# Stick-breaking attention of a streaming encoder step: four chains a head pair, softplus by absolute value, and projections placed behind named transposes

## The chip, the cores and the metric

The kernel runs on one core of one Trainium2 chip. The metric is the device time in microseconds (us) of one execution of the whole program, the median of several runs. A profile is one more execution, recorded by the hardware; its span runs from its first to its last recorded instruction.

A core has engines that run side by side, each with a queue that it takes in order: TensorE (PE, matmuls and transposes, with PEld for its weight loads), VectorE (DVE), ScalarE (ACT), GpSimd (POOL) and SyncE (SP, which here only starts DMA transfers). Operands lie in SBUF; TensorE writes to PSUM, eight banks of 128 x 512 floats.

## The reference: what is computed

A two-layer encoder takes one step for 512 prompt tokens and 8 running streams of 16 tokens (T = 640 rows of 1024). Each layer is half an FFN, a mixer, half an FFN. The change lies in the first layer's mixer, in its attention of 8 heads of 64 columns. The prompt has only its own keys; a running stream also has 256 cached keys and values.

```
def sb_block(q_blk, q_pos, k, v):
    z = einsum('bqhd,bkhd->bhqk', q_blk, k) * (SB_HEAD_DIM ** -0.5)
    mask = arange(k.shape[1])[None, :] < q_pos[:, None]
    sp = where(mask, softplus(z), 0.0)
    suffix = cumsum(sp, axis=3, reverse=True) - sp
    w = where(mask, exp(log_sigmoid(z) - suffix), 0.0)
    return einsum('bhqk,bkhd->bqhd', w, v)
...
    proj = x @ w_in                       # u for the S5 part; q, k, v
    g = gelu(ys + d_skip * u)             # ys: the S5 recurrence
    s5_out = g * sigmoid(g @ w_glu + b_glu)
    out = concatenate([s5_out, sb_out]) @ w_out
```

Since log_sigmoid(z) = z - softplus(z), a weight is exp(z - the sum of softplus from this key to the last).

## The kernel before

**Products.** Every fp32 projection is three products of fp32r halves: `split` (L93) casts the high part on ScalarE (L94) and subtracts it on VectorE (L95); `mm3` (L128) multiplies high by high, low by high and high by low (L133). `load_w` loads a weight and splits it.

**Attention.** The eight heads are four pairs p. `in_qk(p)` (L1050) projects a pair's q and k: each of the two weights takes 24 matmuls of 256 columns, then 24 of 384. `attend(p, i)` is the chain of prompt queries 128i to 128i+127, of n = 128(i+1) keys, both heads at once: scores (L962) and mask (L965) into two PSUM banks z; softplus in four steps (min on VectorE L951, Exp and Ln on ScalarE through `act_fn` L82, max on VectorE L954); a suffix sum for each head (L970); z minus the sums (L972); Exp; transposes back into z (L977); a copy to SBUF on ScalarE (L978); the weighted sum of the values (L981). Four such chains a pair, of 2 x 128 to 2 x 512 columns. `sample(p)` is the running streams' chain: their new keys are turned round by two matmuls with copies between (L995, L998); then come two halves f of four streams each, one after the other: scores (L1009, L1010, L1012), softplus, sum, subtraction, Exp, three transposes (L1021), a copy on VectorE (L1022); then the weighted sums of both (L1030, L1034), a copy (L1037) and transposes back (L1040, L1044).

**Places.** There are two z buffers of two banks each, three banks `a` for projections and one bank `o` for weighted sums. The cached keys `kc` have one buffer, the cached values `vc` three.

**Fill.** TensorE has other work to do while a chain runs on the other engines: `in_qk` of later pairs, the gate `s5_wglu` (8 groups of 12 matmuls), and the first half of the output projection, `out_half(0, t)` (10 groups of 12 matmuls of 512 columns, each added to `yacc` at L903). The second half, `out_half(4, t)`, needs the whole attention and ends the stage.

**Order.** A scheduler sets each engine's order before the program runs, by the program's order and by what waits for what; on the chip every engine takes its queue in that order. `tc.issue_after(x)` puts an instruction behind x in that order. In the kernel before nothing in this stage uses it.

Of the kernel before, what the change touches and what calls it, by code (L numbers as in the profile page):

```python
# [21 lines left out]
T = 640  # L22
# [13 lines left out]
def kernel(ctx: ExitStack, tc: tile.TileContext, I, O, phases=PHASES):  # L36
# [691 lines left out]
    def mixer0(ph, last):  # L728
# [167 lines left out]
        def out_half(k0, t):  # L896
            ks = range(k0, k0 + 4)
            for j in range(2):
                pb = bank_a()
                mm3(pb, [(xh[:, k, t * 128:t * 128 + 128], xl[:, k, t * 128:t * 128 + 128]) for k in ks],  # L900
                    [w_j(wo[k], j) for k in ks])
                ya = yacc[:, t, j * 512:j * 512 + 512]
                V.scalar_tensor_tensor(ya, pb, 1.0 / ALPHA, ya, op0=ALU.mult, op1=ALU.add)  # L903

        with ExitStack() as st:
# [50 lines left out]
            def attend(p, i, qT, kT, po):  # L956

                n = 128 * i + 128
                z = bank_z()
                for h in range(2):  # L960
                    rows = slice(64 * h, 64 * h + 64)
                    nc.tensor.matmul(z[:, h, :n], qT[rows, n - 128:n], kT[rows, :n],  # L962
                                     start=True, stop=False, skip_group_check=True)
                for h in range(2):
                    nc.tensor.matmul(z[:, h, n - 128:n], identb, negc, start=False, stop=True, skip_group_check=True)  # L965
                e = wk.tile([128, 2, 512], F32, name="es", bufs=4)
                S = wk.tile([128, 2, 512], F32, name="S", bufs=2)
                softplus_(e[:, :, :n], z[:, :, :n])
                for h in range(2):
                    V.tensor_tensor_scan(S[:, h, :n][:, ::-1], onec[:, 0:1].to_broadcast([128, n]),  # L970
                                         e[:, h, :n][:, ::-1], 0.0, op0=ALU.mult, op1=ALU.add)
                V.tensor_tensor(S[:, :, :n], z[:, :, :n], S[:, :, :n], op=ALU.subtract)  # L972
                act_fn(S[:, :, :n], S[:, :, :n], AF.Exp)

                for h in range(2):
                    for j in range(i + 1):
                        nc.tensor.transpose(z[:, h, 128 * j:128 * j + 128], S[:, h, 128 * j:128 * j + 128], ident)  # L977
                nc.scalar.copy(e[:, :, :n], z[:, :, :n])  # L978
                for j in range(i + 1):
                    for h in range(2):  # L980
                        nc.tensor.matmul(po[64 * h:64 * h + 64, n - 128:n],  # L981
                                         vt[:, j, 128 * p + 64 * h:128 * p + 64 * h + 64],
                                         e[:, h, 128 * j:128 * j + 128],
                                         start=(j == 0), stop=(j == i), skip_group_check=True)

            def sample(p, qT, kT):
# [6 lines left out]
                pk = bank("o")  # L993
                zs = bank_z()
                nc.tensor.transpose(pk[:, 0:128], kT[:, 512:640], ident)  # L995
                kk = wk.tile([128, 2, 128], F32, name="kk", bufs=1)
                nc.scalar.copy(kk[:, 0], pk[:, 0:128])
                nc.tensor.matmul(pk[:, 128:256], kk[:, 0], anti, start=True, stop=True)  # L998
                nc.scalar.copy(kk[:, 1], pk[:, 128:256])
                sp = wk.tile([128, 2, 512], F32, name="es", bufs=4)[:, :, :384]  # L1000
# [664 lines left out]
```

## Time and profile before

| | us |
|---|---|
| three runs, median | 2598.07 |
| lowest, highest | 2596.40, 2602.76 |
| the profiled execution, its time | 2599.58 |
| its span | 2597.9 |
| its mean granted TensorE clock | 0.988 |

The rows of the profile stand in a section below. The page's first line gives, for each engine, its busy time, its share of the span and its number of instructions. A window row gives the same for a stretch of time, with the granted clock (PEclk, 1.00 is 2.4 GHz, 0.50 is 1.2 GHz). Matmuls follow each other in a pipeline, so their single durations add up to more than the time they take; how long a series takes is read from its starts.

### The profile page before, as it was taken

The page shows a single profiled execution, that of the slowest core. Times are in us where ns is not written, and L with a number is a line of the kernel's source. Part 1 is how long each engine was busy: PE and PEld are TensorE (multiplying, and loading weights), DVE is VectorE, ACT ScalarE, POOL GpSimd, SP SyncE. Part 2 cuts the span into 40 slices and gives each one's busy share as a digit, 9 for nine tenths or more (in the row PEclk, how much of TensorE's full clock was granted, in tenths as well). Part 3 has the DMA queues.
Part 4 walks back from the last instruction along what each step waited for, and adds up shares of the span by engine and source line. Part 5 has one row for each costly group of instructions (what it writes and reads, how often), then busy time and mean ns, then how long its engine had stood idle before and what let it go on. Part 6 is the DMA issues. An engine that isn't in the chain of part 4 may idle for free. (4 is left out here: it accounts for less than half of the span.)

```text
span 2597.9 us, 40706 instructions
## 1 busy us (share of the span) xinstructions
PE 2522.9 (97%) x15577; PEld 2297.7 (88%) x15577; DVE 2038.0 (78%) x3728; ACT 1213.9 (47%) x2332; POOL 290.2 (11%) x412
## 2 busy tenths in 40 slices
PE   8999999999969999999999999999999999999998
PEld 8999998887648999998999999889899878999997
DVE  7788877667757988887888887777777698876768
ACT  4443444345534454554355554566565443443332
POOL 0000002110012000003000001411121151000001
PEclk9999999999979999999999999999999999999999
DMA  5332334542221244443144335355564622443442
GB/s 181 106 106 83 114 110 139 168 150 85 77 69 49 65 126 110 110 126 107 57 110 116 106 95 161 91 183 175 181 200 138 230 94 76 153 154 113 142 137 94
DMA packets 174835, 317.44 MB, mean 122 GB/s; under 512 B 20480, under 2 KB 91776, under 8 KB 174128
## 3 DMA queue, kind: packets, MB, share of 16 engines
q1 hardware_dynamic: 164816, 293.83, 35.5%
q0 software_dynamic: 9824, 21.01, 4.0%
q8 instruction: 122, 2.00, 0.3%
q14 instruction: 73, 0.60, 0.1%
HBM read 259.56 MB, written 40.54 MB: 116 GB/s over the span
## 5 line engine op out<-in xcount | busy, mean ns | idle before, releaser
L95 DVE TENSOR_TENSOR w<-raw,w 128x512 fp32r<-128x512 f32 (+1 forms) x617 | 537.0, 894 | 89.7 <-ACT w L94 87.7
L94 ACT CAST w<-raw 128x512 fp32r<-128x512 f32 (+1 forms) x617 | 451.1, 772 | 290.6 <-PE bank L133 111.3
L133 PE MATMUL bank<-xhi,w 128*128 128x256 f32 (+2 forms) x2528 | 557.6, 312 | 14.1 <-ACT xhi L94 6.9
L355 PE MATMUL bank<-xhi,w 128*128 128x320 f32 x2432 | 540.0, 309 | 1.7 <-ACT mx L366 1.4
L133 PEld LDWEIGHTS bank<-xhi,w 128*128 128x128 f32 x2528 | 423.1, 189 | 26.3 <-ACT xhi L94 8.0
L133 PE MATMUL bank<-w,h 128*128 128x512 f32 x1872 | 435.3, 391 | 0.8 <-DVE w L95 0.8
L355 PE MATMUL bank<-T,w 128*128 128x320 f32 x2736 | 426.3, 309 | 1.8 <-DVE s L392 1.3
L133 PEld LDWEIGHTS bank<-w,h 128*128 128x128 f32 x1872 | 349.3, 188 | 73.4 <-DVE w L95 1.2
L355 PEld LDWEIGHTS bank<-xhi,w 128*128 128x128 f32 x2432 | 407.4, 188 | 5.6 <-ACT mx L366 2.5
L355 PEld LDWEIGHTS bank<-T,w 128*128 128x128 f32 x2736 | 406.4, 188 | 3.6 <-DVE s L392 2.2
L133 PE MATMUL bank<-xlo,w 128*128 128x256 f32 (+2 forms) x1264 | 392.5, 311 | 6.4 <-DVE xlo L95 6.4
L355 PE MATMUL bank<-xlo,w 128*128 128x320 f32 x1216 | 375.0, 308 | 0.0
L133 PEld LDWEIGHTS bank<-xlo,w 128*128 128x128 f32 x1264 | 239.2, 189 | 8.9 <-DVE xlo L95 7.6
L355 PEld LDWEIGHTS bank<-xlo,w 128*128 128x128 f32 x1216 | 228.0, 188 | 0.3
L208 DVE SCALAR_TENSOR_TENSOR yacc<-bank,yacc 128x512 f32<-128x512 f32 x160 | 109.4, 687 | 76.3 <-PE bank L133 75.6
L366 ACT COPY mx<-bank 128x320 f32<-128x320 f32 x228 | 96.4, 423 | 141.4 <-PE bank L355 140.8
L95 DVE TENSOR_TENSOR w<-sw,w 128x1024 fp32r<-128x1024 f32 x76 | 93.0, 1224 | 53.2 <-ACT w L94 52.9
L94 ACT CAST w<-sw 128x1024 fp32r<-128x1024 f32 x76 | 79.8, 1050 | 101.2 <-DVE sw L334 100.0
L499 POOL DMA_DIRECT2D yacc<-ev x56 | 48.7, 903 | 651.5 <-ACT ev L498 597.5
L133 PE MATMUL bank<-w,og 128*128 128x512 f32 x432 | 106.3, 400 | 2.8 <-DVE og L1459 2.8
L133 PEld LDWEIGHTS bank<-w,og 128*128 128x128 f32 x432 | 80.7, 191 | 21.1 <-DVE og L1459 4.7
L394 ACT ACTIVATE s<-s 128x320 f32<-128x320 f32 x108 | 50.8, 470 | 85.3 <-DVE s L392 85.1
(418 smaller groups left out, 3317.7 us busy)
## 6 DMA issues: line engine op xcount, KB each, us to landing
raw<-in_w_gate_dram SPq DMA_DIRECT2D x88, 512.0 KB, 3.9
raw<-in_w_up_dram SPq DMA_DIRECT2D x88, 512.0 KB, 3.9
raw<-in_w_down_dram SPq DMA_DIRECT2D x88, 512.0 KB, 3.6
raw<-in_m_in_dram SPq DMA_DIRECT2D x52, 512.0 KB, 4.6
yacc<-ev POOLq DMA_DIRECT2D x56, 256.0 KB, 4.3
raw<-in_m_out_dram SPq DMA_DIRECT2D x24, 512.0 KB, 3.9
csb<-cs_d SPq DMA_DIRECT2D x20, 512.0 KB, 5.4
h<-in_ssd_h_dram SPq DMA_DIRECT2D x16, 512.0 KB, 6.1
```

What stands on the lines that cost most here:

```text
L94: nc.scalar.copy(hi, src)
L95: return nc.vector.tensor_tensor(lo, src, hi.bitcast(F32), op=ALU.subtract)
L133: state["pe"] = nc.tensor.matmul(ps, a, b, start=(k == 0), stop=(k == n - 1)).ins
L208: state["acc"] = nc.vector.scalar_tensor_tensor(ya, pb, scale, ya, op0=ALU.mult, op1=ALU.add).ins
L355: nc.tensor.matmul(ps, A[p][:, a, k * 128:k * 128 + 128], B[p][b][:, k, :], start=(first and n == 0), stop=(n == 11), skip_group_check=True)
L366: nc.scalar.copy(e[n], ps)
L394: state["silu"] = nc.scalar.activation(t, ps, AF.Silu).ins
L499: nc.gpsimd.dma_start(yacc[:, t, 512 * j:512 * j + 512], e, accum_op=ALU.add)
```

## The change

- **Chains.** A pair's prompt chains are now three: queries 384 to 511, queries 256 to 383, and the other two blocks side by side in one z buffer (256 + 128 columns a head). The two halves of the running streams are one chain of 2 x 384 columns. Below, u0, u1, u2 and the streams' chain (3 in `mark`) are a pair's four chains in order.
- **Softplus** is max(z, 0) + ln(1 + exp(-|z|)): Abs, Exp with scale -1 and Ln on ScalarE, and one fused operation on VectorE.
- **New keys** are turned round at the pair's start, in a bank `a`. The streams' copies are on ScalarE; their weighted sums go into the free columns of their own z banks. `kc` has two buffers, `es` three.
- **Fill.** `in_qk(1)` moves behind the first pair's chains in the program, `in_qk(2)` and `in_qk(3)` behind the first chain of pairs 1 and 2, and their groups, those of the gate and of the output's first half are each held behind the last transpose of a named chain.

```diff
+            def in_qk(p, places=None):
...
-                        nc.scalar.mul(t[:, o:o + L], cm_proj(wt, h)[:, :L], sc)
+                        with tc.issue_after(mark[places[0]]) if places and mark.get(places[0]) else ExitStack():
+                            pqk = cm_proj(wt, h)
+                        places = places and places[1:]
+                        nc.scalar.mul(t[:, o:o + L], pqk[:, :L], sc)
...
             def softplus_(e, z):
-                V.tensor_scalar_min(e, z, 40.0)
-                act_fn(e, e, AF.Exp)
+                nc.scalar.activation(e, z, AF.Abs)
+                act_fn(e, e, AF.Exp, scale=-1.0)
                 act_fn(e, e, AF.Ln, bias=1.0)
-                V.tensor_tensor(e, z, e, op=ALU.max)
+                V.scalar_tensor_tensor(e, z, 0.0, e, op0=ALU.max, op1=ALU.add)
...
+            def attend(p, u, parts, qT, kT, po):
+                n = sum(128 * i + 128 for i, _ in parts)
+                z = bank_z()
+                for i, o in parts:
+                    for h in range(2):
+                        rows = slice(64 * h, 64 * h + 64)
+                        nc.tensor.matmul(z[:, h, o:o + 128 * i + 128], qT[rows, 128 * i:128 * i + 128],
+                                         kT[rows, :128 * i + 128], start=(o == 0), stop=False, skip_group_check=True)
...
+                    for c in range(0, n, 128):
+                        mark[p, u] = nc.tensor.transpose(z[:, h, c:c + 128], S[:, h, c:c + 128], ident).ins
+                nc.scalar.copy(e, z[:, :, :n])
...
+            def new_keys(kT):
+                pk = bank_a()
+                nc.tensor.transpose(pk[:, 0:128], kT[:, 512:640], ident)
+                kk = wk.tile([128, 2, 128], F32, name="kk", bufs=2)
+                nc.scalar.copy(kk[:, 0], pk[:, 0:128])
+                nc.tensor.matmul(pk[:, 128:256], kk[:, 0], anti, start=True, stop=True)
+                nc.scalar.copy(kk[:, 1], pk[:, 128:256])
+                return kk[:, 1]
...
             in_qk(0)
-            in_qk(1)
             for p in range(4):
...
+                kr = new_keys(kT)
                 po = bank("o")
-                for i in range(4):
-                    attend(p, i, qT, kT, po)
+                for u, parts in enumerate((((3, 0),), ((2, 0),), ((1, 0), (0, 256)))):
+                    attend(p, u, parts, qT, kT, po)
+                    if (p, u) == (1, 0):
+                        in_qk(2, [(0, 2), (0, 3), (0, 3), (1, 0)])
+                    elif (p, u) == (2, 0):
+                        in_qk(3, [(1, 1), (1, 2), (1, 3), (2, 0)])
...
                 V.tensor_copy(qT[:, 0:512], po)
+                if p == 0:
+                    in_qk(1, [None, (0, 0), (0, 1), (0, 2)])
...
             wgl = [load_w(I["s5_wglu"][i]) for i in range(2)]
+            after = [mark[2, n] for n in (0, 1, 1, 1, 2, 2, 3, 3)]
...
+            after = [mark[p, n] for p, n in ((2, 3), (2, 3), (3, 0), (3, 0), (3, 1), (3, 1), (3, 2), (3, 2), (3, 3), (3, 3))]
             for t in range(NT):
-                out_half(0, t)
+                out_half(0, t, after)
```

The following rows are queues of instructions in the order in which TensorE takes them; several equal ones in a row are one row with their count. L133 is a projection (fill) in both kernels. In the changed kernel L968 and L972 are scores and masks, L986 a chain's transposes, L991 its weighted sum, L999 and L1002 the new keys, L1033 the streams' transposes, L1043 and L1047 their weighted sums, L1053 the transposes back.

**First pair.** TensorE before, around the first chain's transposes (L977, a chain of 2 x 128 columns); ahead of this piece stand 24 matmuls of fill:
```order
L133 MATMUL bank<-xhi,w 128x384 x2
L133 MATMUL bank<-xlo,w 128x384
L977 MATMUL bank<-ident,S 128x128 x2
L133 MATMUL bank<-xhi,w 128x384 x2
L133 MATMUL bank<-xlo,w 128x384
L981 MATMUL bank<-es,vt 64x128 x2
L962 MATMUL bank<-kT,qT 128x384 x2
L977 MATMUL bank<-ident,S 128x128 x4
L965 LDWEIGHTS identb
```

TensorE in the changed kernel, around the first chain's transposes; ahead of this piece stand the second chain's scores and masks and 21 matmuls of fill:
```order
L133 MATMUL bank<-xhi,w 128x256 x2
L133 MATMUL bank<-xlo,w 128x256
L986 MATMUL bank<-ident,S 128x128 x13
L991 MATMUL bank<-es,vt 64x128 x8
L986 MATMUL bank<-ident,S 128x128
L968 MATMUL bank<-kT,qT 128x256 x2
L968 MATMUL bank<-kT,qT 128x128
L991 MATMUL bank<-es,vt 64x128 x6
```

The first chain is now the widest, of 2 x 512 columns. Its eight transposes and the six of the second chain stand in a row, with the first chain's weighted sum and then the third chain's scores behind them and no fill between.

**Second pair.** TensorE before, ahead of the transposes of its third chain (2 x 384 columns), with 45 more matmuls of fill in front of this piece:
```order
L133 MATMUL bank<-xhi,w 128x256 x2
L133 MATMUL bank<-xlo,w 128x256
L977 MATMUL bank<-ident,S 128x128 x6
L133 MATMUL bank<-xhi,w 128x256 x2
L133 MATMUL bank<-xlo,w 128x256
L133 MATMUL bank<-xhi,w 128x256 x2
```

TensorE in the changed kernel, ahead of the transposes of its second chain (2 x 384 columns); in front of this piece stand the scores of the second and third chains:
```order
L972 LDWEIGHTS identb
L972 MATMUL bank<-negc,identb 128x128
L999 MATMUL bank<-ident,kT 128x128
L1002 MATMUL bank<-anti,kk 128x128
L986 MATMUL bank<-ident,S 128x128 x6
L133 MATMUL bank<-xhi,w 128x256 x2
L133 MATMUL bank<-xlo,w 128x256
L986 MATMUL bank<-ident,S 128x128 x3
L991 MATMUL bank<-es,vt 64x128 x6
```

The fill ahead of these transposes is gone from this place: all of the third pair's projections now stand in front of the second chain's scores. Ahead of the transposes there are only scores, masks and the new keys.

**The end.** TensorE before, from the last pair's third chain to the first half of its streams:
```order
L977 MATMUL bank<-ident,S 128x128 x6
L981 MATMUL bank<-es,vt 64x128 x6
L977 MATMUL bank<-ident,S 128x128 x8
L981 MATMUL bank<-es,vt 64x128 x8
L995 MATMUL bank<-ident,kT 128x128
L998 MATMUL bank<-anti,kk 128x128
L1009 MATMUL bank<-kk,qb 128x128
L1010 LDWEIGHTS identb
L1010 MATMUL bank<-negs,identb 128x128
L1012 MATMUL bank<-kc,qb 32x256 x4
L1021 MATMUL bank<-ident,es 128x128 x3
L1009 MATMUL bank<-kk,qb 128x128
```

TensorE in the changed kernel, around the last pair's streams' chain:
```order
L133 MATMUL bank<-w,xhi 128x512 x2
L1033 MATMUL bank<-ident,S 128x128 x6
L133 MATMUL bank<-w,xlo 128x512
L133 MATMUL bank<-w,xhi 128x512 x2
L133 MATMUL bank<-w,xlo 128x512
L1043 MATMUL bank<-vrev,es 128x128
L1047 MATMUL bank<-vc,es 32x128 x8
L1043 MATMUL bank<-vrev,es 128x128
L1047 MATMUL bank<-vc,es 32x128 x4
L133 MATMUL bank<-w,xhi 128x512 x2
L133 MATMUL bank<-w,xlo 128x512
L133 MATMUL bank<-w,xhi 128x512 x2
```

Before, no projection stands between the last chains' steps; now the output products of the first half stand around the streams' transposes and weighted sums.

## Rows read from the trace of the kernel before

**Rows 1.** The page's span and busy line: engine, busy us, share, instructions.
```profile
span 2597.9 us, 40706 instructions
...
PE 2522.9 (97%) x15577; PEld 2297.7 (88%) x15577; DVE 2038.0 (78%) x3728; ACT 1213.9 (47%) x2332; POOL 290.2 (11%) x412
```

**Rows 2.** Windows over the stage: stretch, us, busy by engine, PEclk, DMA.
```profile
570.80:584.60 13.80, 13.80 (x97) 13.61 (x96) 2.59 (x4) 3.80 (x8) 0.00 (x0) 1.00 0.44 139
584.60:722.60 138.00, 129.16 (x910) 96.79 (x909) 105.30 (x167) 79.88 (x150) 2.21 (x6) 0.98 0.26 80
722.60:759.60 37.00, 16.52 (x112) 10.05 (x112) 18.89 (x27) 12.24 (x20) 1.17 (x2) 0.57 0.32 101
759.60:803.70 44.10, 44.10 (x258) 38.62 (x257) 32.42 (x59) 16.12 (x25) 21.79 (x17) 0.98 0.12 34
```

**Rows 3.** VectorE's groups, 584 to 762: count | busy us, mean ns | idle before.
```profile
L970 DVE TENSOR_TENSOR_SCAN S<-onec,es 128x512 f32<-128x512 f32 x8 | 9.3, 1208 | 0.0
...
L970 DVE TENSOR_TENSOR_SCAN S<-onec,es 128x384 f32<-128x384 f32 x8 | 7.2, 942 | 0.0
L903 DVE SCALAR_TENSOR_TENSOR yacc<-bank,yacc 128x512 f32<-128x512 f32 x10 | 6.6, 683 | 0.8 <-PE bank L133 0.8
...
L951 DVE TENSOR_SCALAR es<-bank 128x1024 f32<-128x1024 f32 x4 | 4.9, 1214 | 0.5 <-PE bank L965 0.5
L954 DVE TENSOR_TENSOR es<-bank,es 128x1024 f32<-128x1024 f32 x4 | 4.8, 1208 | 0.0
...
L954 DVE TENSOR_TENSOR es<-bank,es 128x768 f32<-128x768 f32 x4 | 3.8, 953 | 3.6 <-ACT es L82 3.6
```

**Rows 4.** ScalarE's groups by shape, the same stretch.
```profile
L94 ACT CAST w<-raw 128x512 fp32r<-128x512 f32 x22 | 12.4, 615 | 1.6 <-PE bank L133 1.6
L82 ACT ACTIVATE es<-es 128x1024 f32<-128x1024 f32 x8 | 8.4, 1056 | 3.3 <-DVE es L951 3.1
L82 ACT ACTIVATE es<-es 128x768 f32<-128x768 f32 x8 | 6.7, 840 | 0.7 <-DVE es L951 0.5
...
L978 ACT COPY es<-bank 128x1024 f32<-128x1024 f32 x4 | 4.1, 1013 | 6.8 <-PE bank L977 6.8
```

**Rows 5.** TensorE's timeline: start us, us, what, output and operands, count.
```profile
570.80 0.39 PE L133 MATMUL bank<-xhi,w 128*128 128x256 f32 x2
...
577.68 0.39 PE L133 MATMUL bank<-xhi,w 128*128 128x256 f32 x2
...
580.41 0.51 PE L133 MATMUL bank<-xhi,w 128*128 128x384 f32 x2
...
584.66 0.49 PE L962 MATMUL bank<-kT,qT 64*128 64x128 f32 x4
...
586.03 0.48 PE L133 MATMUL bank<-xhi,w 128*128 128x256 f32 x2
...
762.23 0.39 PE L133 MATMUL bank<-w,xlo 128*128 128x512 f32 x1
...
764.97 0.39 PE L133 MATMUL bank<-w,xlo 128*128 128x512 f32 x1
```

**Rows 6.** Windows around stretches at the lower clock, columns as in Rows 2.
```profile
645.70:648.60 2.90, 2.90 (x20) 2.35 (x19) 2.39 (x6) 2.29 (x5) 0.00 (x0) 0.50 0.20 24
690.00:693.80 3.80, 3.80 (x17) 3.02 (x17) 0.96 (x2) 1.01 (x1) 0.00 (x0) 0.57 0.41 126
728.00:759.00 31.00, 14.37 (x91) 8.50 (x91) 13.48 (x20) 7.07 (x14) 1.17 (x2) 0.50 0.34 111
803.70:806.00 2.30, 0.07 (x1) 0.00 (x0) 1.42 (x4) 0.28 (x1) 0.00 (x0) 0.99 0.83 283
806.00:812.50 6.50, 3.89 (x12) 3.90 (x13) 3.92 (x9) 1.89 (x4) 0.00 (x0) 0.50 0.09 35
```

**Rows 7.** A wait of TensorE (timeline, idle in brackets); the cached values' landing.
```profile
808.61 1.97 PE L133 MATMUL bank<-xhi,w 128*128 128x384 f32 x5 [4.83 <-ACT xhi L94]
...
DMA to landing us min/median/max: 2.9/4.4/5.6
```

More of the change, by code (lines that the diff above doesn't have):

```diff
@@ L899, in out_half @@
                 pb = bank_a()
-                mm3(pb, [(xh[:, k, t * 128:t * 128 + 128], xl[:, k, t * 128:t * 128 + 128]) for k in ks],
-                    [w_j(wo[k], j) for k in ks])
+                with tc.issue_after(marks.pop(0)) if marks else ExitStack():
+                    mm3(pb, [(xh[:, k, t * 128:t * 128 + 128], xl[:, k, t * 128:t * 128 + 128]) for k in ks],
+                        [w_j(wo[k], j) for k in ks])
                 ya = yacc[:, t, j * 512:j * 512 + 512]
@@ L992, in sample @@
                 qbf = qb.rearrange("p f b h i -> p f (b h i)")
-                pk = bank("o")
                 zs = bank_z()
[L995 to L1000, printed above, removed]
@@ L1011, in sample @@
                     for j in range(4):
[L1012 removed]
+                        nc.tensor.matmul(z[32 * j:32 * j + 32, f, 128:384], qbf[:, f, 32 * j:32 * j + 32], kc[:, j, :],
                                          start=False, stop=(j == 3), skip_group_check=True)
[L1014 to L1015 removed]
+                e, S = places(384)
@@ L1016, in sample @@
+                softplus_(e, z)
+                for f in range(2):
+                    V.tensor_tensor_scan(S[:, f], onec[:, 0:1].to_broadcast([128, 384]), e[:, f], 0.0,
                                          op0=ALU.mult, op1=ALU.add)
-                    V.tensor_tensor(sp[:, f], z, S[:, f], op=ALU.subtract)
-                    act_fn(sp[:, f], sp[:, f], AF.Exp)
-                    pt = z.rearrange("p (k r) -> p k r", r=128)
+                V.tensor_tensor(S, z, S, op=ALU.subtract)
+                act_fn(S, S, AF.Exp)
@@ L1020, in sample @@
+                for f in range(2):
                     for k in range(3):
-                        nc.tensor.transpose(pt[:, k, :], sp[:, f, 128 * k:128 * k + 128], ident)
-                    V.tensor_copy(wT[:, f], pt)
-                po = pk[:, 256:512].rearrange("p (f c) -> p f c", c=128)
+                        c = slice(128 * k, 128 * k + 128)
+                        mark[p, 3] = nc.tensor.transpose(z[:, f, c], S[:, f, c], ident).ins
+                nc.scalar.copy(e, z)
+                wT = e.rearrange("p f (k r) -> p f k r", k=3)
@@ L1024, in sample @@
+                po = zs[:, :, 384:512]
                 for f in range(2):
@@ L1034, in sample @@
                             nc.tensor.matmul(po[32 * j:32 * j + 32, f], wT[:, f, 1 + k, 32 * j:32 * j + 32],
-                                             vcs[k][:, j, :], start=False, stop=(f == 1 and k == 1),
-                                             skip_group_check=True)
-                nc.scalar.copy(pvs, po[:, 0:2])
-                pt = pk[:, :256]
+                                             vcs[k][:, j, :], start=False, stop=(k == 1), skip_group_check=True)
+                pvs = wk.tile([128, 2, 128], F32, name="pvs", bufs=1)
+                nc.scalar.copy(pvs, po)
+                pt = zs[:, 0, 0:256]
                 for f in range(2):
@@ L1082, in mixer0 @@
                     ps_ = bank_a()
-                    mm3(ps_[:, :L],
-                        [w_k(wgl[m // 2], 4 * (m % 2) + k) for k in range(4)],
-                        [(xh[:, k, o:o + L], xl[:, k, o:o + L]) for k in range(4)])
+                    with tc.issue_after(after.pop(0)):
+                        mm3(ps_[:, :L],
+                            [w_k(wgl[m // 2], 4 * (m % 2) + k) for k in range(4)],
+                            [(xh[:, k, o:o + L], xl[:, k, o:o + L]) for k in range(4)])
                     s = wk.tile([128, 384], F32, name="gs", bufs=1)[:, :L]
```

89 lines of the change are left out of this document (41 added, 48 removed).

## The prediction, made before the change was run

> **What bounds the kernel now.** I read first the page's busy line [rows 1]: TensorE is busy for 97% of the span, so time can be had only where it waits or runs slowly. Then the stretches of the first mixer's attention [rows 2]. The stage begins at 570.8, when the first pair's q and k have been multiplied, and ends at 759.6, when the second half of the output projection begins. In its first 13.8 us TensorE never waits; in the next 138.0 it is busy for 129.2; in the last 37.0 for 16.5, and there the granted clock is 0.57. The last pair's chains, with nothing left to put between them, are that tail. After 759.6 TensorE is busy without a break for 44.1 us. So the stage's end is what the change can move.
>
> TensorE's own work, as if all at full clock, is 13.8 + 125.8 + 9.2 = 148.8 us. For the middle I take 129.2 less half of the 2.9 and 3.8 us that the clock stood low [rows 6]; for the tail the 16.5 us, of which 14.4 fall into the half-clock stretch and so count half [rows 6]. The stage takes 188.8 us, so 40 us are lost; another 1.0 is lost behind 759.6, until the clock is back. Least possible: 148.8 us, a gain of 41.
>
> Then the prices: VectorE and ScalarE operations by shape [rows 3, 4], TensorE's steps [rows 5], the clock [rows 6], the waits and the landing of a cached-values load [rows 7].
>
> **Softplus.** Before, VectorE does min, ScalarE Exp and Ln, VectorE max. Now ScalarE does Abs, Exp, Ln, and VectorE one fused max-and-add. Per 1024 columns the min's 1.21 us [rows 3] becomes an Abs that the trace doesn't show; its bounds are the copy out of the same bank, 1.01, and the Exp, 1.06 [rows 4]; I take 1.06. The fused operation lies between the max it replaces, 1.21, and twice the 512-column one of the same kind, 2 x 0.68 = 1.37 [rows 3]; I take 1.21, the same two operands of the same size. So a chain gets 0.2 us shorter at most. VectorE loses 5.5 us of work a pair (five minima, two copies), ScalarE gains about 4.4; neither sets the end: in the middle they are busy for 105 and 80 of 138 us [rows 2].
>
> The min took VectorE 1.21 us, Exp and copy of the same 1024 columns took ScalarE 1.06 and 1.01 [rows 3, 4]. The Trainium skill (Trainium Architecture — The Big Picture, The five engines, in one table) speaks against the move: it calls ScalarE wrong for simple arithmetic, since VectorE is up to about three times faster per element. These rows don't agree.
>
> **Chains.** A chain is scores, softplus, two suffix sums, subtraction, Exp, transposes, copy, weighted sum. The blocks of 256 and 128 queries become one chain, and the two halves of the running streams too: their second set of seven waits goes. In the tail that is one whole chain, run at half clock.
>
> **Order, where I part from the change's aim.** Nothing is taken from TensorE; what matters is what it has to do while a chain runs on ScalarE and VectorE. The fill is now bound to stand behind transposes, and the new order shows what that does at a pair's start: scores, then the transposes of the same chain, nothing between. I follow the new order with the rows' durations.
>
> First pair. After its scores TensorE has the next chain's scores and 24 matmuls of 256 columns: 1.2 + 2.7 = 4.0 us [rows 5]. The chain needs Abs 1.06, Exp 1.06, the next chain's Abs ahead of Ln 0.85, Ln 1.06, max-add 1.21, two sums 2.4, the next chain's max-add 0.95, subtraction 1.21, Exp 1.06: 10.9 [rows 3, 4]. TensorE waits 6.9 us. Before, the first chain was the short one (256 columns).
>
> Second pair. All of the third pair's q and k is put ahead of the second and third chains' scores, so no chain runs beside its last 8 us. Then come scores and scores, 1.9 us with masks, and the first of two key-reversal steps. The chain needs the rest of a weight cast 0.35, Abs 0.85, Exp 0.85, the other Abs 0.85, Ln 0.85, max-add 0.95, two sums 1.9, the other max-add 0.95, subtraction 0.95, Exp 0.84 [rows 3, 4]: 9.3. Wait: 9.3 - 1.9 - 0.4 = 7.0. Third pair, the same with 12 matmuls of 256 columns, 1.4 us, between: 5.6. Last pair, 4.5 us of fill between, but four weight casts (some 2.4 us, [rows 4]) stand ahead of the chain's last Exp on ScalarE, of which I let 1.4 fall into time in which it waits for VectorE anyway; 9.0 + 1.0 - 1.9 - 0.4 - 4.5 = 3.2. Sum of the four: 22.7.
>
> Smaller waits by the same walk: start of the stage 0.8; first pair's second chain 0.8; third chains, 0.9 each in three pairs and 2.0 in the last (its copy stands behind a cast that waits for VectorE): 4.6; the streams' transposes, 2.5, 1.0 and 0.9 in the first three pairs: 4.4; a product bank that VectorE gives back late: 3.3.
>
> One wait is new in kind. The values of the running streams come in four loads into three buffers. The fourth load can start only when the first buffer has been read, and the weighted sum for it now stands about 3.4 us later, in the middle of the next chain's transposes. A load lands after 2.9 to 5.6 us, median 4.4 [rows 7]: 0.7 to 1.2 us a pair, 4.2 in all; nothing if all land in 2.9, twice that at 5.6. Behind it on TensorE's queue are the last transposes, and behind those the copy and the weighted sum.
>
> Waits: 22.7 + 0.8 + 0.8 + 4.6 + 4.4 + 3.3 + 4.2 = 40.8 us.
>
> Clock. A wait of 4.8 us brought the clock from full to half 2.3 us after it began, and it stayed there for 3.9 us of work after the wait [rows 6, 7]; half of that, 2 us, is lost. Five of the waits are long enough (the four, and the 2.5); with part of the work behind a second wait I take 1.6 each: 8.1.
>
> The last pair is the good part. Its streams' chain now runs beside output products, ten of 2.75 us [rows 5], and only 1.7 and 1.1 us of waiting are left there.
>
> **Sum.** In the walk the two heads' scores of the first chain stand apart and cost 1.1 more; fewer switches between kinds of matmul I put at 2.7 less: 147.2 + 40.8 + 8.1 = 196.1 us against 188.8 + 1.0. That is 6.3 us more. Behind the stage I expect no change: the last two output weights are cast only when the first half ends, one step ahead of use. The profiled execution took 2599.6 us (span 2597.9 and 1.7 around it), 1.5 above the median of 2598.1; on the profile I expect 2606, on the median 2604. So the tail's loss is spread over four pairs rather than removed. 0.3%, about what a measurement can tell from no change, is 7.8 us.
>
> **Rivals.**
> 1. Slower: the clock stays down through each pair's start. For: from 728 to 759, where TensorE was busy for 14.4 of 31 us in pieces, it stood at 0.50 throughout [rows 6]. At a pair's start about 5 us of transposes, weighted sums and scores are broken by waits of about 1 us, then 4.6 us of fill. If all of it and the fill run at 1.2 GHz, 4 us more in pairs two and three, 2 in the others: 12, so 2616. Against: 690 to 693.8, where steady work brought it back after 3.8 us. [...] The Trainium skill (TensorE: Matmul & The Clock Gate, HAM oscillation) tells of a loop whose bursts between waits run at the low clock; the tail of this trace does that.
> 2. The change does what it is for: each chain finds cover, as most do before. Then only the middle's losses stay, some 9 us of waits and 3 of clock, and the tail's 28 go: 2570. Against: the order has no fill between scores and transposes in pairs two and three, and an engine takes its queue in order.
> 3. All doubtful prices fall to their low ends: loads land in 2.9 us (-4.2), the 2.5 us wait does not move the clock (-1.5), casts are out of the way (-1.5), waits at the banks go (-3). 2594.
> 4. The new Abs costs three times the min: 3.6 us for 1024 columns, 2.9 for 768, on the path once in the first pair and twice in the others: 2.6 + 3 x 4 = 14 more, 2618. The rows speak against it. It is the rule of the Trainium skill's table of engines, named above.
>
> **Numbers.** Forecast 2604 (its own range 2596 to 2610): 52 in 100. Rival 1: 27. Rival 2: 9. Rival 3: 10. Rival 4: 2. About a fifth of the forecast's cases lie above 2605.9. Slower by over 0.3%: 27 + 2 + 10 = 39. Faster: 9 + 4 from the edge of rival 3 = 13. Within: 48. The range goes from 2588 to 2619: it leaves out rival 2 and the far end of rival 1.
>
> **What would show it.** Right: TensorE idle for 5 to 7 us before the transposes of the first chain of pair one and of the second chain of pairs two and three, released by ScalarE's Exp; the clock at half behind each; no idle of over 2 us between the last streams' chain and the stage's end; the stage ending 196 us after it began. Wrong: waits under 3 us at those places, an Abs far from 1.06, or more than 44 us between the stage's end and the next long wait.

## The result and the profile after

The changed kernel takes 2608.6 us (median of six runs, 2604.05 to 2610.78) against 2597.8: a ratio of 1.0037, 95% interval 1.0024 to 1.0050. It is slower by 11 us (0.4%); 2604 (6 us slower) was forecast, in a range of 2588 to 2619. Its profiled execution took 2609.62 us, 10.0 more than that of before.

The page of the changed kernel, its busy line, answers [rows 1]; TensorE's busy time is the same to 0.6 us:

```profile
span 2607.9 us, 40669 instructions
...
PE 2523.5 (97%) x15577; PEld 2302.8 (88%) x15577; DVE 2016.0 (77%) x3681; ACT 1223.4 (47%) x2325; POOL 289.9 (11%) x412
```

Its windows answer [rows 2] and [rows 6]: the whole stage from the end of the first pair's projections to the end of the output's first half, the second half, and the four stretches behind the pairs' long waits; then two more stretches, behind two shorter waits of the first and third pair (columns as in [rows 2]; the last but two is the granted clock):

```profile
572.34:767.67 195.33, 160.26 (x1116) 125.68 (x1116) 102.58 (x147) 104.19 (x168) 3.07 (x8) 0.90 0.23 74
767.67:812.10 44.43, 43.25 (x256) 37.91 (x256) 35.20 (x63) 17.67 (x29) 21.80 (x17) 1.00 0.25 76
...
586.50:594.10 7.60, 7.04 (x38) 5.45 (x38) 1.56 (x2) 2.58 (x4) 0.00 (x0) 0.51 0.00 1
645.90:653.30 7.40, 6.73 (x42) 5.09 (x44) 1.89 (x4) 2.33 (x3) 0.00 (x0) 0.59 0.00 0
687.30:696.00 8.70, 8.04 (x43) 5.75 (x45) 2.13 (x5) 2.33 (x4) 0.00 (x0) 0.50 0.00 0
726.40:734.20 7.80, 6.16 (x39) 4.20 (x41) 6.25 (x12) 4.32 (x9) 0.00 (x0) 0.56 0.27 85
...
618.90:624.00 5.10, 4.97 (x47) 3.85 (x48) 3.76 (x4) 1.86 (x2) 0.00 (x0) 1.00 0.22 64
709.90:713.60 3.70, 3.66 (x21) 2.85 (x21) 1.23 (x3) 2.12 (x5) 0.00 (x0) 0.54 0.53 155
```

The stage lasts 195.3 us instead of 188.8; TensorE waits for 195.33 - 160.26 = 35.1 of them. Behind each of the four long waits it runs for 7 to 9 us near 1.2 GHz; what the low clock cost there, estimated from each busy time and clock, is 7.04 x 0.49 + 6.73 x 0.41 + 8.04 x 0.50 + 6.16 x 0.44 = 12.9 us. The tail is gone: from 726.5 to the stage's end TensorE waits once for more than 1 us.

TensorE's timeline of the changed kernel: the rows of the stage with a wait of over 1.5 us (in brackets, with what ended it), and the two behind the stage:

```profile
586.59 1.97 PE L986 MATMUL bank<-ident,S 128*128 128x128 f32 x8 [6.65 <-ACT S L82]
...
618.90 0.87 PE L1033 MATMUL bank<-ident,S 128*128 128x128 f32 x6 [2.68 <-ACT S L82]
...
641.41 0.57 PE L1002 MATMUL bank<-anti,kk 128*128 128x128 f32 x2 [3.14 <-ACT kk L1001]
645.95 1.54 PE L986 MATMUL bank<-ident,S 128*128 128x128 f32 x6 [3.97 <-ACT S L82]
...
682.56 0.49 PE L1002 MATMUL bank<-anti,kk 128*128 128x128 f32 x2 [1.77 <-ACT kk L1001]
687.36 1.54 PE L986 MATMUL bank<-ident,S 128*128 128x128 f32 x6 [4.31 <-ACT S L82]
...
726.50 1.08 PE L986 MATMUL bank<-ident,S 128*128 128x128 f32 x6 [3.57 <-ACT S L82]
729.12 1.55 PE L991 MATMUL bank<-es,vt 128*64 128x128 f32 x12 [1.54 <-ACT es L987]
...
768.85 0.51 PE L133 MATMUL bank<-w,xhi 128*128 128x512 f32 x1 [1.18 <-DVE yacc L904]
...
817.25 1.97 PE L133 MATMUL bank<-xhi,w 128*128 128x384 f32 x5 [5.12 <-ACT xhi L94]
```

These are the places that the prediction named: the first chain of the first pair (6.65), the second chain of the second (3.14 + 3.97, in two parts, since the second step of the next pair's new keys stands in the queue between and waits for a copy that ScalarE has behind the softplus), of the third (1.77 + 4.31) and of the last (3.57).

Where the 10.0 us of the two profiled executions lie: 1.5 ahead of the stage (it starts at 572.34 instead of 570.80), 6.8 from there to the next long wait (before it began at 808.61 - 4.83 = 803.78, now at 817.25 - 5.12 = 812.13), 1.7 behind. The first part isn't the change's. TensorE takes the same matmuls in the same order up to there in both kernels, and the windows behind a wait that both have (3.06 us before, 2.61 after) show the same work at another clock, before first, then after:

```profile
471.70:498.00 26.30, 26.28 (x173) 24.78 (x173) 11.01 (x22) 7.04 (x14) 0.54 (x2) 0.94 0.54 184
```
```profile
471.70:498.00 26.30, 26.28 (x166) 25.11 (x167) 9.47 (x19) 7.03 (x14) 0.00 (x0) 0.88 0.50 173
```

### The profile page after: what moved, and what is told of

It is laid out like the page before. It is cut to its first block, busy times and chain, and to the rows that moved or that the text cites. A ratio compares the mean times of both kernels' runs of the same rounds, so it can differ in the third digit from the quotient of the medians.

```text
span 2607.9 us, 40669 instructions
## 1 busy us (share of the span) xinstructions
PE 2523.5 (97%) x15577; PEld 2302.8 (88%) x15577; DVE 2016.0 (77%) x3681; ACT 1223.4 (47%) x2325; POOL 289.9 (11%) x412
## 5 line engine op out<-in xcount | busy, mean ns | idle before, releaser
L133 PE MATMUL bank<-xhi,w 128*128 128x256 f32 (+2 forms) x2528 | 560.8, 314 | 16.2 <-ACT xhi L94 8.3
L133 PEld LDWEIGHTS bank<-xhi,w 128*128 128x128 f32 x2528 | 425.1, 190 | 28.9 <-ACT xhi L94 9.4
L133 PE MATMUL bank<-w,h 128*128 128x512 f32 x1872 | 435.1, 390 | 0.8 <-DVE w L95 0.8
L133 PEld LDWEIGHTS bank<-w,h 128*128 128x128 f32 x1872 | 349.2, 188 | 73.2 <-DVE w L95 1.2
L133 PE MATMUL bank<-xlo,w 128*128 128x256 f32 (+2 forms) x1264 | 393.2, 312 | 6.1 <-DVE xlo L95 6.1
L133 PEld LDWEIGHTS bank<-xlo,w 128*128 128x128 f32 x1264 | 240.1, 190 | 8.4 <-DVE xlo L95 7.3
L133 PE MATMUL bank<-w,og 128*128 128x512 f32 x432 | 104.8, 396 | 2.8 <-DVE og L1489 2.8
L133 PEld LDWEIGHTS bank<-w,og 128*128 128x128 f32 x432 | 79.6, 188 | 20.6 <-DVE og L1489 4.6
```

Of the source, the lines that this page charges most:

```text
L133: state["pe"] = nc.tensor.matmul(ps, a, b, start=(k == 0), stop=(k == n - 1)).ins
```

## The experiments

The theory (A): a chain costs TensorE its own length less the fill that stands in its queue ahead of the chain's transposes; the change puts the fill elsewhere, and each long wait is paid again by the clock. Rivals: B, the waits only move, because wide chains leave too little to do; C, the softplus on ScalarE is at fault. Each kernel below ran beside the kernel before on the same chip, and its ratio is to those runs; the kernels ran on several chips, so two of them are compared by their ratios.

| kernel | us | ratio to before | 95% interval |
|---|---|---|---|
| changed kernel | 2608.6 | 1.0037 | 1.0024 to 1.0050 |
| e1_untied | 2573.5 | 0.9907 | 0.9893 to 0.9921 |
| e2_moved | 2589.4 | 0.9968 | 0.9956 to 0.9980 |
| e3_oldsoftplus | 2603.3 | 1.0022 | 1.0013 to 1.0030 |
| e4_before_abs | 2595.1 | 0.9987 | 0.9979 to 0.9996 |
| e5_fillties | 2595.6 | 0.9992 | 0.9981 to 1.0004 |
| e6_busywait | 2592.5 | 0.9983 | 0.9975 to 0.9992 |
| e7_fiveuntied | 2574.3 | 0.9917 | 0.9902 to 0.9933 |
| e8_earlyqk | 2578.6 | 0.9932 | 0.9918 to 0.9947 |
| e9_halves | 2576.8 | 0.9927 | 0.9914 to 0.9939 |
| e10_fivebufs | 2565.3 | 0.9885 | 0.9871 to 0.9898 |
| e11_fourbufs | 2563.7 | 0.9879 | 0.9864 to 0.9894 |
| e12_sharedbank | 2584.2 | 0.9960 | 0.9946 to 0.9973 |

**e1_untied.** Nothing is held back any more:

```diff
-                        with tc.issue_after(mark[places[0]]) if places and mark.get(places[0]) else ExitStack():
+                        with ExitStack():
...
-                    with tc.issue_after(after.pop(0)):
+                    with ExitStack():
...
-                out_half(0, t, after)
+                out_half(0, t)
```

> The changed kernel with all three kinds of holding back removed (projections, gate groups and output products are no longer put behind a named transpose); chains, softplus and the places in the program stay. In the order that results, TensorE has 8.0 us of fill ahead of the first chain's transposes of pair 0 (2.7 before), 6.0 us ahead of the second chain's of pair 1 (none), 4.4 us in pair 2 (1.4) and 7.3 us in pair 3 (4.5). Theory A (the waits at the pairs' starts, 6.65, 7.1, 6.1 and 3.6 us in the changed kernel's trace, are there because the fill stands elsewhere): they fall to about 1.4, 1.0, 2.6 and 0.8 us, 17.7 us less, and the low clock behind them gives back 5 to 10 us: 2576 to 2590 us. Rival B (three wide chains leave too little for TensorE to do, wherever the fill stands; the waits only move): 2602 to 2614 us.

2573.5 us, by the ratios 34 less than the changed kernel and 24 less than the kernel before; that is 2.5 under theory A's range and far from rival B's. The stage's window, then TensorE's timeline: the first chain's transposes, all waits of over 0.7 us up to 670, and the waits before the second chain's transposes in the second and the last pair:

```profile
569.90:733.70 163.80, 151.34 (x1117) 118.70 (x1116) 102.79 (x147) 103.25 (x168) 3.95 (x8) 0.97 0.28 88
```
```profile
584.26 1.06 PE L986 MATMUL bank<-ident,S 128*128 128x128 f32 x8
...
626.96 0.49 PE L1002 MATMUL bank<-anti,kk 128*128 128x128 f32 x2 [0.76 <-ACT kk L1001]
...
631.50 0.87 PE L986 MATMUL bank<-ident,S 128*128 128x128 f32 x6 [0.40 <-ACT S L82]
...
645.79 0.88 PE L1033 MATMUL bank<-ident,S 128*128 128x128 f32 x6 [1.22 <-ACT S L82]
...
651.36 0.66 PE L986 MATMUL bank<-ident,S 128*128 128x128 f32 x4 [0.73 <-ACT S L82]
...
665.07 1.12 PE L986 MATMUL bank<-ident,S 128*128 128x128 f32 x6 [2.58 <-ACT S L82]
667.51 1.55 PE L991 MATMUL bank<-es,vt 128*64 128x128 f32 x12 [1.32 <-ACT es L987]
...
703.13 0.87 PE L986 MATMUL bank<-ident,S 128*128 128x128 f32 x6 [0.58 <-ACT S L82]
```

The first chain's transposes at 584.26 have no wait in front (6.65 in the changed kernel), the second pair waits 0.76 + 0.40, the third 2.58, the last 0.58: 4.3 instead of 23.4. All waits together fall from 35.1 to 12.5, and TensorE's busy time falls from 160.3 to 151.3 with the same instructions, since the clock is 0.97 instead of 0.90. So the waits don't move: B falls.

**e2_moved.** The ties stay; two projections are written at another place:

```diff
-                    if (p, u) == (1, 0):
+                    if (p, u) == (1, 2):
                         in_qk(2, [(0, 2), (0, 3), (0, 3), (1, 0)])
-                    elif (p, u) == (2, 0):
+                    elif (p, u) == (2, 2):
                         in_qk(3, [(1, 1), (1, 2), (1, 3), (2, 0)])
```

> The changed kernel with the projections of the third and fourth pair written behind the pair's last prompt chain instead of behind its first; everything stays held back as it was. The order then has the second and third chains' scores first and 6.4 us (pair 1) and 6.5 us (pair 2) of projections between them and the second chain's transposes, 5.7 in pair 3; pair 0 is as in the changed kernel. Theory A: the waits of pairs 1 and 2 fall from 7.1 and 6.1 to about 1 us each, pair 3's from 3.6 to 2.4, pair 0's 6.65 stays; with the clock 2588 to 2597 us. Rival B: 2602 to 2614 us.

2589.4 us, inside theory A's range. TensorE's timeline at the four places:

```profile
584.71 1.97 PE L986 MATMUL bank<-ident,S 128*128 128x128 f32 x8 [6.65 <-ACT S L82]
...
635.63 0.88 PE L986 MATMUL bank<-ident,S 128*128 128x128 f32 x6 [0.85 <-ACT S L82]
...
669.87 0.88 PE L986 MATMUL bank<-ident,S 128*128 128x128 f32 x6 [0.85 <-ACT S L82]
...
706.32 0.87 PE L986 MATMUL bank<-ident,S 128*128 128x128 f32 x6 [2.49 <-ACT S L82]
```

6.65, untouched, is there to the last digit; pairs two and three wait 0.85 each, the last 2.49. Where the fill stands decides, whichever means puts it there.

**e5_fillties.** Only the gate's and the output's ties are removed (the second and third hunk of e1's diff).

> The changed kernel with the projections still held back as in the change, but the gate groups and output products free. In the order pairs 0 and 1 are as in the changed kernel (waits of 6.65 and 7.1 us stay), pair 2 has 5.5 us of fill ahead of its second chain's transposes instead of 1.4, pair 3 7.3 instead of 4.5. Theory A (each wait is the chain's length less the fill that stands in front of its transposes): 6.1 falls to about 2, 3.6 to about 0.8, 7 us less, and some 4 to 6 of clock: 2594 to 2600 us. Rival B (waits move): 2602 to 2614.

2595.6 us, inside theory A's range. TensorE's timeline, the waits before the second chain's transposes in the second, third and last pair:

```profile
635.79 0.80 PE L1002 MATMUL bank<-anti,kk 128*128 128x128 f32 x2 [3.15 <-ACT kk L1001]
640.33 1.54 PE L986 MATMUL bank<-ident,S 128*128 128x128 f32 x6 [3.74 <-ACT S L82]
...
678.08 0.49 PE L1002 MATMUL bank<-anti,kk 128*128 128x128 f32 x2 [0.75 <-ACT kk L1001]
...
682.88 0.87 PE L986 MATMUL bank<-ident,S 128*128 128x128 f32 x6 [1.24 <-ACT S L82]
...
718.74 0.87 PE L986 MATMUL bank<-ident,S 128*128 128x128 f32 x6 [0.59 <-ACT S L82]
```

The second pair waits 3.15 + 3.74, nearly as in the changed kernel, the third 0.75 + 1.24 and the last 0.59. The first waits 5.23, where 6.65 was expected: the clock stood at 0.81 from 567.2 to 576.3, so the same fill took longer and covered more of the chain. The two sorts of ties share the loss: taken away in this order, those of the gate and the output are worth 0.45% (12 us) by the ratios and those of the projections 0.85% (22 us).

**e3_oldsoftplus, e4_before_abs.** The softplus is put back in the changed kernel, or put alone into the kernel before:

```diff
-                nc.scalar.activation(e, z, AF.Abs)
-                act_fn(e, e, AF.Exp, scale=-1.0)
+                V.tensor_scalar_min(e, z, 40.0)
+                act_fn(e, e, AF.Exp)
                 act_fn(e, e, AF.Ln, bias=1.0)
-                V.scalar_tensor_tensor(e, z, 0.0, e, op0=ALU.max, op1=ALU.add)
+                V.tensor_tensor(e, z, e, op=ALU.max)
```

> The changed kernel with softplus in its old four steps (min on VectorE, Exp, Ln, max). Theory A (softplus does not matter for the time, an Abs costs ScalarE what the min costs VectorE to within 0.2 us): within 4 us of the changed kernel, 2604 to 2612; a little less is possible since the order puts 7.3 instead of 4.5 us of fill at the start of pair 3. Rival C (the work moved to ScalarE holds up the chains): 2598 us or less.

> The kernel before with the new softplus alone. Theory A: the same as before to 0.2%, at most 3 us faster, since a chain gets up to 0.2 us shorter and the tail has three of them in a row: 2594 to 2601. Rival C: 2603 us or more.

2603.3 and 2595.1 us. The first lies 0.7 us under theory A's range and 5 over rival C's; the second is inside theory A's. With the old softplus the long waits are still there (6.31; 1.47 + 5.68; 0.87 + 5.47), but the order that comes out has 7.3 us of fill in the last pair and a wait of 0.90 there instead of 3.57. By the ratios this kernel is 4 us faster than the changed one, and the two intervals overlap; the other order goes with it, so this run doesn't tell what the softplus by itself is worth there. In the kernel before, the new softplus alone gains 3 us (ratio 0.9987, interval 0.9979 to 0.9996). C falls: where it stands alone the softplus is worth 0.1%, for the good.

**e6_busywait.** This asks what a wait costs beyond its own length. Useless matmuls, whose result nothing reads, are put into the second part of the waits of pairs two and three:

```diff
-                nc.tensor.matmul(pk[:, 128:256], kk[:, 0], anti, start=True, stop=True)
+                k2 = nc.tensor.matmul(pk[:, 128:256], kk[:, 0], anti, start=True, stop=True).ins
+                with tc.issue_after(k2):
+                    for _ in range(extra):
+                        nc.tensor.matmul(pk[:, 256:384], kk[:, 0], ident, start=True, stop=True)
...
-                kr = new_keys(kT)
+                kr = new_keys(kT, (0, 0, 14, 15)[p])
```

> The changed kernel with 14 and 15 useless matmuls (a spare corner of the new keys' bank, never read) put into the second part of the long waits of pairs 1 and 2, where TensorE stood idle for 3.97 and 4.31 us; at 0.22 us each they fill 3.1 and 3.3 us and nothing waits for them. The order of the rest is nearly the same; pair 3 gets 6.2 instead of 4.5 us of fill by it, worth up to 1.7 us and perhaps 1 of clock. Theory A1 (the second cost of a wait is the low clock after it: 0.59 for 7.4 us in pair 1 and 0.50 for 8.7 us in pair 2, some 6.8 us lost): TensorE stays at or comes back to the full clock earlier, 2599 to 2604 us. Rival (the stretches behind the waits are slow for another reason than the idleness, or the first 3.1 and 1.8 us of waiting are enough to bring the clock down for as long): 2605 to 2609 us, the rows behind the two waits at 0.5 as now.

2592.5 us, by the ratios 0.54% (14 us) less than the changed kernel, for doing more; that is below both expectations, on theory A1's side by 6.5 us. The new keys' second step, the useless matmuls and the transposes behind them in pair three; then the windows behind the transposes in both pairs, which answer the windows at 645.90 and 687.30 above:

```profile
674.90 0.49 PE L1002 MATMUL bank<-anti,kk 128*128 128x128 f32 x2 [1.77 <-ACT kk L1001]
675.23 3.51 PE L1005 MATMUL bank<-ident,kk 128*128 128x128 f32 x30
679.70 0.87 PE L986 MATMUL bank<-ident,S 128*128 128x128 f32 x6 [0.96 <-ACT S L82]
```
```profile
640.00:650.00 10.00, 10.00 (x98) 7.58 (x97) 3.88 (x7) 5.49 (x8) 0.58 (x2) 1.00 0.23 79
679.00:690.00 11.00, 9.95 (x94) 7.46 (x95) 4.89 (x9) 6.74 (x10) 0.58 (x2) 1.00 0.31 91
```

From the second step to the transposes it is 4.80 us, as in the changed kernel (682.56 to 687.36): the chain itself is no faster (in pair two it is 4.85 instead of 4.54, since the useless matmuls there end late). But the clock stands at 1.00 where it was 0.59 and 0.50. From the first of these transposes to the last mask of the next pair's first scores it is 7.5 and 7.9 us instead of 10.1 and 11.5, 6.2 together. In the profiled executions the stage is 11.1 us shorter (184.20 instead of 195.33); of the other 4.9 us, 4.0 lie behind the last of these masks, in the last pair, where 1.7 us of fill moved and the wait fell from 3.57 to 1.62. So 6.2 us are shown as the price of the clock behind two waits, and no more. The ratios differ by 14 us; what the last 3 are these runs don't tell.

**e7_fiveuntied, e9_halves.** Without ties, the merged chains are taken apart again: the blocks of 256 and 128 queries in e7, the streams' two halves too in e9:

```diff
-                for u, parts in enumerate((((3, 0),), ((2, 0),), ((1, 0), (0, 256)))):
+                for u, parts in enumerate((((3, 0),), ((2, 0),), ((1, 0),), ((0, 0),))):
```

In e9, softplus, sum, subtraction, Exp, transposes and copy also stand inside the loop over f.

> The changed kernel with nothing held back and with the blocks of 256 and 128 queries as two chains again (four prompt chains a pair; the streams' halves stay together). It tells what merging these two blocks is worth: theory A, little where the fill covers the chains anyway, one hand-over set more a pair: within 0.3% of the untied kernel's 2573.5, 2570 to 2582 us. Rival D (the merging of the prompt's blocks is the main gain of the untied kernel): 2584 to 2598 us.

> The kernel with nothing held back and five... four prompt chains a pair (e7_fiveuntied), and with the two halves of the running streams as two chains again, one behind the other. No chain is merged any more; what is left of the change is the new softplus, the new keys at the pair's start, the widest block first, the later place of the projections and the second buffer for the cached keys. Theory A (a chain costs TensorE only what the fill does not cover, and here 0.5 to 4.6 us of fill and other chains' steps stand ahead of each half's transposes against 4.2 us of chain): 2574 to 2584 us. Rival D (fewer chains are the gain): 2588 to 2600 us, as the kernel before with the new softplus alone (2595).

2574.3 and 2576.8 us, both inside theory A's ranges; ratios 0.9917 and 0.9927 against e1's 0.9907, and the intervals overlap. The order of e9 leaves one wait of 4.71 us, before the second chain's transposes of its third pair. Merging chains is worth nothing that these runs can tell, as long as fill covers them.

**e12_sharedbank.** So what keeps the tail open in the kernel before? In e9 the new keys, the streams' sums and the transposes back go into bank `o` again:

```diff
-                pk = bank_a()
+                pk = bank("o")
...
+                kr, pk = new_keys(kT)
...
-                po = zs[:, :, 384:512]
+                po = pk[:, 256:512].rearrange("p (f c) -> p f c", c=128)
...
-                pt = zs[:, 0, 0:256]
+                pt = pk[:, :256]
...
-                kr = new_keys(kT)
```

The call of `new_keys` moves with it, from the pair's start into `sample`.

> e9_halves with one thing put back as it was before: the new keys, the streams' weighted sums and the transposes back share the single bank `o` with the prompt's weighted sums, so the keys are turned round in `sample` and not at the pair's start. Theory E (what keeps the tail open in the kernel before is this bank: the last pair's streams cannot begin until its prompt sum has been read out, and by then the fill is used up): in the resulting order all output products of the first half stand ahead of the last streams' two halves again, and 0.2 us of fill is left between them; the two halves cost waits as before (4.5, 0.65, 2.8, 0.65, 0.5 in rows of the kernel before, about 9 us) and some 3 to 4 us of low clock: 2586 to 2595 us. Rival (the bank does not matter; the block order and the places of the projections made e9 faster than the kernel before): 2573 to 2581 us.

2584.2 us, 7 to 9 more than e9 (by the medians and by the ratios), between the two expectations and nearer to theory E. The last streams' chains in its timeline, and the window over them:

```profile
731.96 0.90 PE L1032 MATMUL bank<-ident,S 128*128 128x128 f32 x3 [5.72 <-ACT S L82]
733.43 0.80 PE L1020 MATMUL bank<-kk,qb 128*128 128x128 f32 x2 [0.57 <-ACT es L1033]
...
739.79 0.90 PE L1032 MATMUL bank<-ident,S 128*128 128x128 f32 x3 [2.71 <-ACT S L82]
741.26 0.80 PE L1042 MATMUL bank<-vrev,es 128*128 128x128 f32 x2 [0.57 <-ACT es L1033]
...
743.57 0.69 PE L1053 MATMUL bank<-ident,pvs 128*128 128x128 f32 x2 [0.49 <-ACT pvs L1050]
```
```profile
726.00:745.00 19.00, 8.94 (x59) 5.17 (x59) 7.96 (x14) 6.81 (x15) 1.16 (x2) 0.58 0.55 180
```

The two long ones are these in the kernel before:

```profile
747.48 0.90 PE L1021 MATMUL bank<-ident,es 128*128 128x128 f32 x3 [4.52 <-ACT es L82]
...
755.47 0.90 PE L1021 MATMUL bank<-ident,es 128*128 128x128 f32 x3 [2.78 <-ACT es L82]
```

The streams' part of the old tail is back, 10.1 us of waits and the clock at 0.58. In e12 the last streams' keys are turned round only after the last of the prompt's sums (722.93, the sum at 721.28), and by then the fill is nearly gone; in e9 the last streams' first scores stand at 717.50. That is one part of the kernel before's loss. The edit moves the keys' place in the program together with the bank, and the two were not taken apart. e9's wait of 4.71 us isn't in e12, so the difference of the two kernels is less than what the tail costs. The prompt's part of the old tail does not come back here; e12 is still 0.4% (10 us) faster than before, and which of block order, place of the projections or buffers brings that was not taken apart.

**e8_earlyqk.** e1 with the second pair's projections ahead of the first pair:

```diff
             in_qk(0)
+            in_qk(1)
...
-                if p == 0:
-                    in_qk(1, [None, (0, 0), (0, 1), (0, 2)])
```

> The changed kernel with nothing held back and with the second pair's projections written ahead of the first pair again, as in the kernel before. In the order the fill is spread more evenly (3.1 + 4.6 us ahead of the first transposes, 5.0 in pair 3). Theory A: 2567 to 2577 us, the sum of waits about that of the untied kernel (some 12 us). Rival B: the program's place of the fill matters as much as the ties: 2580 us or more.

2578.6 us, between the two expectations: it tells little. Its 0.25% (6 us) over e1, whose interval it just touches, go with waits for cached values (1.28 and 1.73) and for the gate's banks (0.92 and 1.36), which e1's timeline does not show.

**e10_fivebufs, e11_fourbufs.** Two more buffers in e7 and in e1:

```diff
-                        vc = wk.tile([128, 4, 128], F32, name="vc", bufs=3)
+                        vc = wk.tile([128, 4, 128], F32, name="vc", bufs=4)
...
-                    s = wk.tile([128, 384], F32, name="gs", bufs=1)[:, :L]
+                    s = wk.tile([128, 384], F32, name="gs", bufs=2)[:, :L]
```

> e7_fiveuntied with four buffers for the cached values instead of three and two for the gate's scratch tile instead of one. In e7_fiveuntied TensorE waits 0.95 us for cached values and 2.95 us for a product bank that VectorE gives back late while it works on that scratch tile. Theory A: both go, 2567 to 2573 us. Rival: the waits move to other banks and the time stays at 2573 to 2577.

> e1_untied (three prompt chains, nothing held back) with the same two edits, four buffers for the cached values and two for the gate's scratch tile. e1_untied's trace shows no wait on either, so theory A gives no gain from the waits themselves; the order spreads the fill a little differently (4.3 us instead of 2.4 + 3.6 and 4.4 ahead of the second chains): 2569 to 2577 us. Rival: buffers set the time and it falls under 2569.

2565.3 and 2563.7 us: both below what theory A gave, and e11 where its rival put it. e11 is the fastest kernel of this study, 1.2% under the kernel before. Its window over the stage:

```profile
567.75:722.70 154.95, 146.56 (x1112) 115.35 (x1113) 100.62 (x145) 102.13 (x166) 3.75 (x8) 1.00 0.30 91
```

TensorE waits 8.4 us in all, the longest wait is 1.42, and the clock is at 1.00 throughout. e1 had no wait put down to either buffer, so the gain is not a wait taken away at its place: in the order that comes out with the buffers the fill leaves no chain with a wait of over 1.5 us, and the clock stays up. Why the order comes out so was not looked at. It also shows TensorE's own work without loss: 146.6 us.

## Why the prediction was right, and where not

- **Own work.** 147.2 us were forecast; 146.6 is what e11 shows at full clock. Right in sum. Of its two corrections, the 2.7 us for fewer switches between kinds of matmul came from no row, and no run here shows that term by itself.
- **Waits at the pairs' starts.** 6.9, 7.0, 5.6 and 3.2 were forecast; 6.65, 7.11, 6.08 and 3.57 came. Right in place, cause and size. e1 and e2 show the cause: fill between scores and transposes takes them away.
- **Prices of the softplus.** Abs was taken at 1.06 and 0.85 us, the fused operation at 1.21 and 0.95. Rows of the changed kernel, ScalarE and VectorE by shape:

```profile
L953 ACT ACTIVATE es<-bank 128x768 f32<-128x768 f32 x12 | 9.7, 804 | 9.2 <-PE bank L1021 7.0 <-PE bank L972 2.2
...
L953 ACT ACTIVATE es<-bank 128x1024 f32<-128x1024 f32 x4 | 4.1, 1017 | 1.0 <-PE bank L972 1.0
```
```profile
L956 DVE SCALAR_TENSOR_TENSOR es<-bank,es 128x768 f32<-128x768 f32 x12 | 11.4, 949 | 24.7 <-ACT es L82 24.7
...
L956 DVE SCALAR_TENSOR_TENSOR es<-bank,es 128x1024 f32<-128x1024 f32 x4 | 4.9, 1217 | 5.0 <-ACT es L82 5.0
```

  1.02 and 0.80, the price of the copy out of the same bank [rows 4] rather than that of the Exp; 1.22 and 0.95. Rival 4 falls: here ScalarE's Abs is no slower than VectorE's min (1.21, [rows 3]).
- **The cached values' loads: mis-sized.** 4.2 us of waits were forecast from a landing of 4.4; none came. The sum for the fourth load stands at 624.79 in the first pair, some 3.4 us after the first buffer was read (the sums that read it start at 621.08). The landings of all sixteen loads of this run:

```profile
DMA to landing us min/median/max: 2.7/3.5/7.3
```

  The fourth loads of the four pairs landed after 3.0, 3.3, 2.9 and 2.8 us; in the kernel before three of these four took 4.3 to 5.1. So the step that failed is the landing price, taken over from the kernel before; the low end of its range was the right one, and why these loads land sooner here no run shows.
- **Clock: mis-sized the other way.** 8.1 us were forecast; 12.9 came behind the four long waits. The step that failed took 3.9 us of work after a wait for the length of the slow stretch [rows 6]; that held for steady work. At the pairs' starts, where waits of 0.5 to 1.5 us follow the long one, 6 to 8 us of work ran slowly, as rival 1 had it. But the clock came back before the fill that rival 1 let run at half speed, so its full 12 more did not come. The fifth wait that the term counts, 2.5 us forecast and 2.68 measured before the first pair's streams' transposes, cost no clock (1.00 from 618.9 to 624.0). In its place 3.66 us of work ran at 0.54 from 709.9 on, in the third pair, behind three waits of 0.4 to 1.1 us: an estimated 1.7 us that no term had.
- **Sum of the stage.** 196.1 us forecast, 195.3 measured: waits 5.7 too many (above all the cached values' 4.2, and a product bank's 3.3, of which 1.1 came), clock 4.8 too few, or 6.5 with the fifth stretch. The errors cancel; the total is better than its parts, and that is luck. The 1.7 and 1.1 us that the text leaves beside the last streams' chain stand in no term of the sum; 0.5 came there. Behind the stage 1.2 us of waiting for VectorE at the second half's first matmuls was not forecast. With it the stretch from the stage's end to the next long wait is 44.5 us, over the 44 that the prediction named as a sign of being wrong; it was 44.2 before, so that bound left no room.
- **Rival 2** (every chain covered, 2570) did not happen in the changed kernel, but e1 is that case: 2573.5 us. The form of the chains allowed it; the ties took it away.
- **The median** lies 4.6 us over the forecast. The stage and what follows it up to the next long wait account for 6.8 of the 10.0 us between the profiled executions; the rest lies where TensorE has the same queue in both kernels, and these runs don't show that the change has to do with it.

The reason given beforehand, that the loss now lies at the pairs' starts because the fill stands elsewhere, is shown by e1, e2 and e5. It did not have to be spread: in e1 the same chains without ties have neither the tail nor the long waits. That the low clock is a second price of the same waits is shown by e6, for two of them.

## What to carry to other kernels

A tie that holds filler work behind a named instruction also fixes where it cannot be: before adding one, look at what stands in the queue between the step that starts a chain on other engines and the step that waits for it, for every chain. Shortening or merging chains gains little while filler covers them; a bank that two chains share can undo that cover, as far as e12 shows, when the last chain comes to stand behind the filler. And a wait is to be priced with the slow stretch behind it, which here was 2.7 to 4.0 us, estimated from the rows above, on top of each of the four long waits.

## What the runs showed that was not expected

Work that does nothing made the kernel faster: 29 useless matmuls in two waits kept the granted clock at 1.00 instead of 0.59 and 0.50 behind them, and the ratio to the kernel before fell from 1.0037 to 0.9983, in part by fill that moved with them.

The point at which the clock comes back, with the same instructions behind a wait, differed between the two profiled executions: 0.94 and 0.88 over the same 26.3 us ahead of the stage. By these two figures that is 1.6 us, about the 1.5 by which the stage's start moved.
